# A hybrid decoder layer on one core: norm factors by GpSimd's power in place of a square root and a reciprocal

## The chip, the core and the metric

The kernel runs on one core of a Trainium2 chip. The metric is the device time of one execution in microseconds. Before the change it is 2195.67 us, the median of 3 runs (2195.48 to 2197.35).

## What is computed

One decoder layer over 512 positions of width 2048 in float32. The input is normalised and goes through one projection to four mixers (a gated delta rule with four heads, an RG-LRU, a spatial gating unit and a short convolution). The outputs of the mixers are normalised, joined and projected back, and a gated channel mixer follows. What the change touches are the norms of the mixers' outputs:

```python
def rms_norm(x, w):
    y = xf * lax.rsqrt(jnp.mean(xf * xf, axis=-1, keepdims=True) + EPS)
    return y * w
# gated delta rule, one norm per head of 128 channels
o = o * lax.rsqrt(jnp.mean(o * o, axis=-1, keepdims=True) + EPS) * norm_w * silu(z)
# the other three mixers, one norm each over 512 channels
y_b = rms_norm(rglru_mixer(...), grp_norm_w[l, 0])
y_c = rms_norm(sgu_mixer(...), grp_norm_w[l, 1])
y_d = rms_norm(short_conv_mixer(...), grp_norm_w[l, 2])
y = concatenate([y_a, y_b, y_c, y_d]) @ w_out
```

## The kernel before

In the mixers, channels lie on the 128 partitions and the 512 positions along the columns, so a tile is 128x512. TensorE multiplies float32 as three products of a high and a low half (`mul3`, lines 209 to 211): for every piece of weights ScalarE rounds the high half (line 159) and VectorE subtracts it to get the low half (line 160), each over 128x1024. There are four buffers for the high halves and four for the low ones.

The steps of the mixers are put in an order written out by hand (`MIXERS`): the projections of the heads (`kqv`), the preparation of one head beside the sequential scan of the head before it (`scan_prep`), the gates of the other mixers, the norms, and the gates of the heads (`z_gate`). Within that, a planner of the framework orders each engine's instructions; each engine then runs its own in that fixed order and waits with semaphores. The input projection is done column block by column block (`gemm_T`); the output projection of a block of 512 columns takes its 16 row blocks in four quarters, first the RG-LRU's, then the spatial gate's, the short convolution's and the heads'.

A norm factor is one number per position. Since channels lie on partitions, the squares are summed over partitions by TensorE against a matrix of ones (`ones_sum`, lines 230 and 231), which leaves the sum on all 128 partitions: 128x512 in PSUM, in a bank (`fx`) of which there is one. From it `inv_sqrt` (lines 240 to 243) makes the factor over the whole 128x512: ScalarE's square root with scale and bias (line 241), then VectorE's reciprocal (line 242). VectorE multiplies the mixer's tile by its weight and the factor (line 592 for a head, line 614 for the four tiles of a group). `inv_sqrt` is called seven times: `gdn_norm` for heads 0 to 3 (line 591) and `norm4` for groups 0 to 2 (line 612).

Elsewhere factors of one to four columns are made by `col_rsqrt` (lines 141 to 145) and in `gdn_prep` (line 474), with a multiply-add on VectorE and GpSimd's power to -0.5. GpSimd also adds up squares (lines 590 and 607), multiplies in the convolution (743) and in the gates (755), and zeroes the scan's tile vn (553).

The scan of a head (`gdn_scan`) goes back and forth between the engines: TensorE's `pws` needs VectorE's state `St` (lines 574 and 576), TensorE's `pss` needs VectorE's `vn` (line 564). In the preparation TensorE's `pn` needs `N` (line 490). In the spatial gate TensorE's `pso` writes the bank `fx`, which VectorE empties at line 724.

Of the kernel before, what the change touches and what calls it, by code (L numbers as in the profile page):

```python
# [7 lines left out]
F32 = mybir.dt.float32  # L8
F32R = mybir.dt.float32r
BF16 = mybir.dt.bfloat16  # L10
AF = mybir.ActivationFunctionType
ALU = mybir.AluOpType
# [3 lines left out]
P = 128  # L16
S = 512
# [3 lines left out]
EPS = 1e-6  # L21
# [35 lines left out]
def trunk(ctx: ExitStack, tc: tile.TileContext, x, xT, cols, rows, gdn_row, sgu_row, w_in, w_ba,  # L57
          lru_wa, lru_wx, sgu_ws, w_out, ffn_up, ffn_down, out):
    nc = tc.nc
    v, a, g, pe = nc.vector, nc.scalar, nc.gpsimd, nc.tensor  # L60
# [3 lines left out]
    const = ctx.enter_context(tc.tile_pool(name="const", bufs=1))  # L64
# [13 lines left out]
    def new(tag, name, dt=F32):  # L78
        return tp.tile([P, S], dt, tag=tag, name=name, bufs=NBUF[tag])
# [7 lines left out]
    def G(name):  # L87
        return new("g", name)

    def acc(name):  # L90
        return ps.tile([P, S], F32, tag="acc", name=name, bufs=3)
# [11 lines left out]
    def small(shape, name):  # L103
        return sp.tile(shape, F32, tag=name, name=name)
# [12 lines left out]
    def col(name, i=0):  # L117
        o, _ = _OFF[name]
        return colt[:, o + i:o + i + 1]
# [12 lines left out]
    half = const.tile([P, 16], F32, name="half")  # L132
    g.memset(half, -0.5)

    a.activation(out=small([P, 1], "warm"), in_=half[:, 0:1], func=AF.Square)
    epsc = const.tile([P, 1], F32, name="epsc")
    g.memset(epsc, EPS)
    epsq = const.tile([P, 1], F32, name="epsq")
    g.memset(epsq, EPS * EPS * P)

    def col_rsqrt(dst, src, scale):
        t = small([P, 16], "crs")
# [84 lines left out]
    def ones_sum(hi, lo, bank):  # L227

        p = bank("psum")
        pe.matmul(p, lhsT=onesr, rhs=hi, start=True, stop=False)  # L230
        pe.matmul(p, lhsT=onesr, rhs=lo, start=False, stop=True)
        return p

    def sum_all(src, bank, tag="t"):
        hi, lo = new(tag, "shi", F32R), new(tag, "slo", F32R)
        a.copy(out=hi, in_=src)
        v.tensor_tensor(out=lo, in0=src, in1=hi.bitcast(F32), op=ALU.subtract)
        return ones_sum(hi, lo, bank)

    def inv_sqrt(r, p, scale, bias):  # L240
        a.activation(out=r, in_=p, func=AF.Sqrt, scale=scale, bias=bias)
        v.reciprocal(out=r, in_=r)
        return r

    def to_row(rc, bank, m=None, tag="t", e=v):
# [15 lines left out]
    for c in range(DC):  # L261
# [10 lines left out]
        for j in range(4):  # L272
# [4 lines left out]
                                   op0=ALU.mult, op1=ALU.subtract)  # L277
# [115 lines left out]
    for t in range(NTT):  # L393
# [21 lines left out]
                    in1=gcum.rearrange("p t h -> p (t h)"), op=ALU.subtract)  # L415
# [169 lines left out]
    def gdn_norm(h):  # L585

        o = o_h[h]
        sq = G("osq")
        a.activation(out=sq, in_=o, func=AF.Square)
        g.tensor_tensor(out=sq, in0=sq, in1=sts[h]["q2"], op=ALU.add)  # L590
        r = inv_sqrt(sq, sum_all(sq, fx, "g"), 1.0 / P, epsq)
        v.scalar_tensor_tensor(out=o, in0=o, scalar=col("gdn_norm"), in1=r, op0=ALU.mult, op1=ALU.mult)

    def in_turn(*steps):
# [6 lines left out]
    tot = [None] * 3  # L601
# [7 lines left out]

    def norm4(i, tiles):  # L610

        r = inv_sqrt(tot[i], sum_all(tot[i], fx, "g"), 1.0 / S, epsc)
        for j in range(4):
            v.scalar_tensor_tensor(out=tiles[j], in0=tiles[j], scalar=col("grp", 4 * i + j), in1=r,
                                   op0=ALU.mult, op1=ALU.mult)
            y[4 + 4 * i + j] = tiles[j]
# [156 lines left out]
    def group_norm(i):  # L773
        norm4(i, (yb, yc, yd)[i])
# [4 lines left out]
    for step, i in MIXERS:  # L779
        if step == "scan":  # L780
            in_turn(gdn_scan(i, sts[i]))
        else:
            {"kqv": kqv, "scan_prep": scan_prep, "lru_gate": lru_gate, "sgu_load": sgu_load, "sgu_v": sgu_v,
             "sgu_u": sgu_u, "sconv": sconv, "gdn_norm": gdn_norm, "group_norm": group_norm,
             "z_gate": z_gate}[step](*([] if i is None else [i]))
# [78 lines left out]
    for t in range(NTT):  # L864
        p = acc("pwo")
# [8 lines left out]
        for d in range(DC):  # L874
            v.scalar_tensor_tensor(out=x1[t][d], in0=x1[t][d], scalar=ry[:, t:t + 1], in1=xr[t, d],
                                   op0=ALU.mult, op1=ALU.add)
# [10 lines left out]
        for d in range(DC):  # L887
# [3 lines left out]
            if d % 2 == 0:  # L891
# [4 lines left out]
                            in1=colt[:, o + 4 * d:o + 4 * d + 4].rearrange("p (k o) -> p k o", o=1)  # L896
# [33 lines left out]
    for j in range(2):  # L930
# [4 lines left out]
                               op1=ALU.subtract)  # L935
        v.scalar_tensor_tensor(out=b21, in0=b11, scalar=-1.0, in1=b21, op0=ALU.mult,
                               op1=ALU.subtract)
# [216 lines left out]
```

## Time and profile before

| | |
|---|---|
| median of 3 runs | 2195.67 us |
| the profiled execution | 2186.26 us, span 2184.6 us |
| mean granted TensorE clock | 0.995 |
| TensorE busy | 2155.5 us, 99% |
| VectorE busy | 1396.8 us, 64% |
| ScalarE busy | 897.0 us, 41% |
| GpSimd busy | 133.1 us, 6% |

Engines in the profile: PE is TensorE, PEld its weight loads, DVE is VectorE, ACT is ScalarE, POOL is GpSimd, SP is SyncE. A row of the timeline gives the start and the duration in us, the engine, the line, the operation, output<-inputs, the shape and how many were merged; in brackets the idle time of the engine before it, and what ended it. The matmuls are pipelined, so a row of 0.39 us overlaps the next one. The mixers run until about 626 us, the projections and the channel mixer after that.

### The profile page before, as it was taken

Reading aid. Unit: us, or ns where it says so; the run is one execution under the profiler, and the core shown is the slowest. Engines: PE = TensorE matmul, PEld = TensorE weight load, DVE = VectorE, ACT = ScalarE, POOL = GpSimd, SP = SyncE. Lnnn points to the kernel's source line nnn. Section 1 sums busy time; section 2 is a strip of 40 time slices with the busy share of each in tenths; the row PEclk is TensorE's granted clock in tenths of the full one; section 3 lists DMA queues with packets and bytes.
Section 4 is the critical chain, followed back from the end, with each engine's and each line's share of the span. In section 5 each row is a group of like instructions: output and inputs, shape, how many; then the busy total and the mean of one; then the engine's idle time right before and its main releaser. Section 6 shows DMA issues by size and latency. Waiting matters only on the chain.

```text
span 2184.6 us, 32153 instructions
## 1 busy us (share of the span) xinstructions
PE 2155.5 (99%) x13226; PEld 1932.2 (88%) x13226; DVE 1396.8 (64%) x1853; ACT 897.0 (41%) x1223; POOL 133.1 (6%) x191
## 2 busy tenths in 40 slices
PE   8999999999999989999999999999999999999997
PEld 7788888888888888999999999999999888888885
DVE  6775454944462386989999999999999322423333
ACT  6554242522332464444445444444445312422222
POOL 0001000100100110000000000000002000100002
PEclk9999999999999999999999999999999999999999
DMA  9232132232232343344344434433446422432233
GB/s 300 68 87 78 58 86 70 78 86 78 87 140 101 133 138 114 104 121 122 110 127 122 123 106 125 126 115 114 121 129 199 174 97 97 168 112 96 96 115 146
DMA packets 316690, 254.85 MB, mean 117 GB/s; under 512 B 10496, under 2 KB 265216, under 8 KB 316032
## 3 DMA queue, kind: packets, MB, share of 16 engines
q1 hardware_dynamic: 304768, 219.24, 32.6%
q0 software_dynamic: 8320, 27.27, 3.4%
q10 hardware_dynamic: 3456, 6.29, 0.8%
q8 instruction: 103, 1.69, 0.3%
q14 instruction: 43, 0.35, 0.0%
HBM read 232.85 MB, written 19.92 MB: 116 GB/s over the span
## 4 chain that ended last, share of the span: by engine, by line
PE 84%; issue 11%; DVE 1%; ACT 1%; DMA 1%; POOL 1%; SPq 0%; DVEq 0%; POOLq 0%; ACTq 0%
PE pT L210 14%; PE pT L211 14%; PE pT L209 14%; PE pB L211 5%; PE pB L210 5%; PE pB L209 5%; PE pd L210 4%; PE pd L211 4%; PE pd L209 4%; PE pwo L211 3%; PE pwo L210 3%; PE pwo L209 3%; PE ptt L442 1%; PE plx L209 1%; PE plx L210 1%
## 5 line engine op out<-in xcount | busy, mean ns | idle before, releaser
L160 DVE TENSOR_TENSOR wlo<-raw,whi 128x1024 fp32r<-128x1024 f32 x378 | 461.6, 1221 | 472.4 <-ACT whi L159 464.6
L159 ACT CAST whi<-raw 128x1024 fp32r<-128x1024 f32 x378 | 396.6, 1050 | 808.5 <-PE pd L211 293.4
L210 PE MATMUL pT<-act_lo,whi 128*128 128x512 f32 (+1 forms) x1032 | 365.7, 354 | 2.4 <-DVE act_lo L900 2.4
L211 PE MATMUL pT<-act_hi,wlo 128*128 128x512 f32 (+1 forms) x1032 | 365.1, 354 | 0.0
L209 PE MATMUL pT<-act_hi,whi 128*128 128x512 f32 (+1 forms) x1032 | 365.1, 354 | 0.0
L211 PE MATMUL pB<-act_hi,wlo 128*128 128x256 f32 x984 | 278.5, 283 | 0.0
L210 PE MATMUL pB<-act_lo,whi 128*128 128x256 f32 x984 | 278.4, 283 | 0.0
L209 PE MATMUL pB<-act_hi,whi 128*128 128x256 f32 x984 | 278.2, 283 | 0.0
L209 PE MATMUL pT<-eh,whi 128*128 128x256 f32 x984 | 277.1, 282 | 0.0
L210 PE MATMUL pT<-el,whi 128*128 128x256 f32 x984 | 277.1, 282 | 0.0
L211 PE MATMUL pT<-eh,wlo 128*128 128x256 f32 x984 | 276.8, 281 | 0.0
L210 PEld LDWEIGHTS pT<-act_lo,whi 128*128 128x128 f32 x1032 | 196.6, 190 | 27.1 <-DVE act_lo L900 2.7
L209 PEld LDWEIGHTS pT<-act_hi,whi 128*128 128x128 f32 x1032 | 196.4, 190 | 25.3 <-issue 1.0
L211 PEld LDWEIGHTS pT<-act_hi,wlo 128*128 128x128 f32 x1032 | 196.6, 190 | 24.7 <-issue 1.0
L159 ACT CAST whi<-s 128x1024 fp32r<-128x1024 f32 x123 | 129.0, 1049 | 185.9 <-DVE s L978 114.2
L211 PE MATMUL pd<-whi,act_lo 128*128 128x512 f32 x512 | 199.4, 389 | 0.0
L210 PE MATMUL pd<-wlo,act_hi 128*128 128x512 f32 x512 | 199.3, 389 | 0.0
L209 PE MATMUL pd<-whi,act_hi 128*128 128x512 f32 x512 | 198.4, 389 | 0.0
L209 PEld LDWEIGHTS pB<-act_hi,whi 128*128 128x128 f32 x984 | 188.8, 192 | 0.0
L211 PEld LDWEIGHTS pB<-act_hi,wlo 128*128 128x128 f32 x984 | 188.7, 192 | 0.0
L210 PEld LDWEIGHTS pB<-act_lo,whi 128*128 128x128 f32 x984 | 188.7, 192 | 0.0
L209 PEld LDWEIGHTS pT<-eh,whi 128*128 128x128 f32 x984 | 185.6, 189 | 0.0
(368 smaller groups left out, 3531.2 us busy)
## 6 DMA issues: line engine op xcount, KB each, us to landing
raw<-in_ffn_up_dram SPq DMA_DIRECT2D x176, 512.0 KB, 3.9
raw<-in_ffn_down_dram SPq DMA_DIRECT2D x88, 512.0 KB, 3.4
raw<-in_w_in_dram SPq DMA_DIRECT2D x86, 512.0 KB, 3.7
raw<-in_w_out_dram SPq DMA_DIRECT2D x32, 512.0 KB, 3.8
gd<-fcv POOLq DMA_DIRECT2D x44, 256.0 KB, 3.8
act_lo<-gd POOLq DMA_DIRECT2D x32, 256.0 KB, 3.8
xs<-in_xT_dram SPq DMA_DIRECT2D x16, 256.0 KB, 6.2
xn<-in_x_dram SPq DMA_DIRECT2D x16, 256.0 KB, 6.1
```

The source lines that it names most:

```text
L159: a.copy(out=hi, in_=r)
L160: v.tensor_tensor(out=lo, in0=r, in1=hi.bitcast(F32), op=ALU.subtract)
L209: pe.matmul(p, lhsT=lt[0], rhs=rt[0], start=first, stop=False)
L210: pe.matmul(p, lhsT=lt[0], rhs=rt[1], start=False, stop=False)
L211: pe.matmul(p, lhsT=lt[1], rhs=rt[0], start=False, stop=last)
L442: pe.matmul(p[:, TS[t]], lhsT=lhsT[:, TS[t]], rhs=rhs[:, TS[t]], start=True, stop=True)
```

## The change

The constants for the bias go. `inv_sqrt` becomes a multiply-add on VectorE, which reads the sum from PSUM and writes it to SBUF, and a power on GpSimd, in place, with the exponent -0.5 read from one column of `half` for all 512 columns. The callers pass the bias as a number.

```diff
-    epsc = const.tile([P, 1], F32, name="epsc")
-    g.memset(epsc, EPS)
-    epsq = const.tile([P, 1], F32, name="epsq")
-    g.memset(epsq, EPS * EPS * P)
 ...
     def inv_sqrt(r, p, scale, bias):
-        a.activation(out=r, in_=p, func=AF.Sqrt, scale=scale, bias=bias)
-        v.reciprocal(out=r, in_=r)
+        v.tensor_scalar(out=r, in0=p, scalar1=scale, scalar2=bias, op0=ALU.mult, op1=ALU.add)
+        g.tensor_tensor(out=r, in0=r, in1=half[:, 0:1].broadcast_to([P, S]), op=ALU.pow)
         return r
 ...
-        r = inv_sqrt(sq, sum_all(sq, fx, "g"), 1.0 / P, epsq)
+        r = inv_sqrt(sq, sum_all(sq, fx, "g"), 1.0 / P, EPS * EPS * P)
 ...
-        r = inv_sqrt(tot[i], sum_all(tot[i], fx, "g"), 1.0 / S, epsc)
+        r = inv_sqrt(tot[i], sum_all(tot[i], fx, "g"), 1.0 / S, EPS)
```

## Rows read from the trace of the kernel before

**Rows 1.** The page, busy us of each engine, share of the span, instructions.

```profile
PE 2155.5 (99%) x13226; PEld 1932.2 (88%) x13226; DVE 1396.8 (64%) x1853; ACT 897.0 (41%) x1223; POOL 133.1 (6%) x191
```

**Rows 2.** Busy times by stretch: length, PE, PEld, DVE, ACT, POOL, PEclk, DMA, GB/s.

```profile
370.00:626.00 256.00, 256.00 (x1259) 215.49 (x1259) 153.41 (x192) 96.09 (x138) 30.81 (x22) 1.00 0.28 79
```

**Rows 3.** Lines 241 and 242: count, ns min/median/max, first and last start.

```profile
L241 ACT ACT_TABLE_LOAD  x5: 1283/1283/1283, 375.0 to 609.1; - x5
...
L242 DVE RECIPROCAL osq<-osq x4: 3344/3353/3354, 377.0 to 611.1; 128x512 f32<-128x512 f32 x4
...
L242 DVE RECIPROCAL nsq<-nsq x3: 3347/3352/3354, 410.9 to 615.5; 128x512 f32<-128x512 f32 x3
```

**Rows 4.** GpSimd's powers (lines 145, 474) and a GpSimd addition (607), same columns.

```profile
L145 POOL TENSOR_TENSOR brs<-crs,half x4: 539/548/556, 293.2 to 304.5; 128x1 f32<-128x1 f32 x4
...
L474 POOL TENSOR_TENSOR rk<-rk,half x4: 1020/1264/1931, 103.2 to 423.4; 128x4 f32<-128x4 f32 x4
...
L607 POOL TENSOR_TENSOR nsq<-nsq x9: 1284/1294/1730, 175.0 to 558.6; 128x512 f32<-128x512 f32 x9
```

**Rows 5.** Timeline of VectorE and GpSimd, 395 to 402 us.

```profile
395.67 0.68 DVE L319 SCALAR_TENSOR_TENSOR kT<-th,gconv 128x512 f32<-128x512 f32 x1
...
400.71 1.30 POOL L590 TENSOR_TENSOR osq<-osq,q 128x512 f32<-128x512 f32 x1 [8.81 <-ACT osq L589]
400.83 1.72 DVE L319 SCALAR_TENSOR_TENSOR qT<-th,gconv 128x512 f32<-128x512 f32 x1
```

**Rows 6.** Timeline of VectorE around the seven reciprocals.

```profile
377.00 3.35 DVE L242 RECIPROCAL osq<-osq 128x512 f32<-128x512 f32 x1 [0.78 <-ACT osq L241]
...
382.31 0.75 DVE L724 SCALAR_TENSOR_TENSOR so<-pso,colt,bt 128x512 f32<-128x512 f32 x1
...
410.93 3.35 DVE L242 RECIPROCAL nsq<-nsq 128x512 f32<-128x512 f32 x1 [0.29 <-ACT nsq L241]
...
418.52 0.28 DVE L574 COPY St<-pss 128x128 f32<-128x128 f32 x1
...
424.40 3.35 DVE L242 RECIPROCAL nsq<-nsq 128x512 f32<-128x512 f32 x1
...
428.35 0.29 DVE L564 TENSOR_TENSOR vn<-u,pws 64x128 f32<-64x128 f32 x1
...
435.52 1.12 DVE L490 SCALAR_TENSOR_TENSOR N<-pkk,cb,DN 128x128 f32<-128x128 f32 x4
...
524.28 3.35 DVE L242 RECIPROCAL osq<-osq 128x512 f32<-128x512 f32 x1 [1.31 <-ACT osq L241]
...
531.43 0.35 DVE L576 SCALAR_TENSOR_TENSOR St<-St,gl,pss 128x128 f32<-128x128 f32 x1 [1.54 <-PE pss L571]
...
611.14 3.35 DVE L242 RECIPROCAL osq<-osq 128x512 f32<-128x512 f32 x1 [1.66 <-ACT osq L241]
...
615.54 3.35 DVE L242 RECIPROCAL nsq<-nsq 128x512 f32<-128x512 f32 x1 [0.25 <-ACT nsq L241]
...
623.20 1.21 DVE L160 TENSOR_TENSOR wlo<-raw,whi 128x1024 fp32r<-128x1024 f32 x1
```

**Rows 7.** Timeline of TensorE, instructions that need a VectorE step of rows 6.

```profile
386.23 0.50 PE L722 MATMUL pso<-wsT,vt 128*128 128x128 f32 x3
...
420.61 0.39 PE L563 MATMUL pws<-St,wT 128*128 128x128 f32 x2
...
431.10 0.39 PE L571 MATMUL pss<-vn,kg 128*128 128x128 f32 x2
...
438.33 0.61 PE L448 MATMUL pn<-ident,N 128*128 128x128 f32 x4
...
536.04 0.39 PE L563 MATMUL pws<-St,wT 128*128 128x128 f32 x2
...
626.89 1.07 PE L209 MATMUL pwo<-whi,act_hi 128*128 128x512 f32 x4
```

**Rows 8.** Busy times by stretch, columns as in rows 2.

```profile
799.00:814.00 15.00, 11.33 (x61) 10.19 (x62) 14.90 (x21) 8.78 (x15) 0.46 (x1) 0.66 0.00 0
```

## The prediction

> **What bounds the kernel now.** I read the page's engine shares first: TensorE is busy 99% of the span, VectorE 64%, ScalarE 41%, GpSimd 6% [rows 1]. Then the busy times of the one stretch in which all seven norm factors are made, from 370 to 626 us: TensorE is busy for 256.0 of 256 us at full clock, VectorE for 153.4, ScalarE for 96.1, GpSimd for 30.8 [rows 2]. So TensorE is the bound here. Nothing that ScalarE or VectorE saves can shorten this stretch; only what makes TensorE stop can change the time. The question is therefore what the new GpSimd instruction takes, who waits for it, and how far TensorE can run on without that waiter.
>
> **What is removed.** Seven square roots on ScalarE with five table loads of 1.28 us, and seven reciprocals of 3.35 us on VectorE [rows 3], 23.5 us of VectorE in all. TensorE waits for none of them (it has no gap in the stretch), so the gain is put at nothing. Two small memsets at the start go too, also at nothing.
>
> **What is added on VectorE.** Seven multiply-adds that read the sum from PSUM. The trace of before has none; the nearest row is a VectorE step of the same size that reads PSUM, 0.75 us at 382.31 [rows 6]. It stands where the reciprocal stood and is shorter than it.
>
> **What is added on GpSimd.** Seven powers over 128x512. The trace has powers only of one column, 0.548 us (median), and of four columns, 1.020 us for the undisturbed ones [rows 4]. Three more columns cost 0.472 us, 157 ns each. The lower bound is the nearest row of the full size: a GpSimd addition over 128x512, 1.29 us [rows 4]. The upper bound is the power's own slope: 0.548 + 511 x 0.157 = 80.9 us. The two are a factor of 60 apart. I take 80.9 us, because the rows of the same operation are nearer to it than a row of another operation: if the power went at the rate of the addition, four columns could not cost 0.47 us more than one. What could still bring it down is a loop that handles many columns faster than four; that is a rival below.
>
> The Trainium skill, GPSIMD Engine Reference, section 3.1 (Elementwise), puts a two-input GpSimd operation at about 2.6 cycles of 1.2 GHz per element; for 512 columns that is an estimate of 1.1 us, and by it the change would cost nothing. The addition's row bears that rate out, the power's rows do not.
>
> **Who waits.** The power's result goes to VectorE, which runs its instructions in order: behind the waiting multiplication (line 592 or 614) stand the low halves of the weights (line 160), the copies out of PSUM and the small steps of the delta-rule scan, and TensorE waits for those. Even if the planner puts other VectorE work ahead of that multiplication, the ports get in the way: a VectorE step of 0.68 us with two inputs in SBUF took 1.72 us when it began 0.12 us after a GpSimd addition of 1.30 us, ending 0.54 us after that one ended [rows 5]. So I take VectorE as stopped from the start of a power to its end, but for steps that read PSUM. Behind it on GpSimd's own queue stand the sums of squares (line 607), the convolution's multiplication (743), the zeroing of vn (553) and the four-column powers of the next head (474); their readers are behind the same stop. The weight loads on the sync queue go on until their buffers are full.
>
> **The sum.** For each stop I take the last VectorE step before it, and the first TensorE instruction that needs a VectorE step behind it; TensorE stops there. VectorE's order is that of before.
>
> Gated norm of head 0: multiply-add at 377.00, power from 377.75 to 458.7. Next on VectorE are three steps that end 2.7 us after the reciprocal did (the one at 382.31 ends at 383.06) [rows 6], so 461.4. TensorE reaches the instruction that needs the bank which this step empties at 386.23 [rows 7]. Lost: 75.2.
>
> The next three come close together, and GpSimd does one after the other. Group 0: 410.93, power from 411.7 to 492.6; the state copy that TensorE needs at 420.61 [rows 7] ended 4.5 us after the reciprocal (its row is at 418.52 [rows 6]), so 497.1: 76.5 lost. Head 1: the multiply-add is next, power from 497.9 to 578.8; one split of weights (1.2 us, as at 623.20), then the multiply-add for group 1 at 580.0, whose power ends at 661.6. In between only the multiplication of head 1 and the vn step get through, at 581.6; TensorE, which needs vn at 431.10, is 150.5 behind. N, needed at 438.33, ended 8.0 us after vn [rows 6, 7], so 669.6: 231.3 behind for the three.
>
> Head 2: 524.28, power from 525.0 to 605.9, then the steps up to the state copy. That ended 4.2 us after the reciprocal, of which 1.5 was a wait for TensorE and 0.3 the vn step, which comes through earlier; I take 2.2, so 608.1. TensorE needs it at 536.04 [rows 6, 7]. Lost: 72.1.
>
> Head 3 and group 2: 611.14, power to 692.8, the multiplication, the second multiply-add, power from 694.3 to 775.2. The first weights of the output projection's third quarter were split 5.5 us after the second reciprocal ended (the row at 623.20 [rows 6]), so 780.7. TensorE has work for the first two quarters until 626.89 [rows 7]. Lost: 153.8.
>
> Together 75.2 + 231.3 + 72.1 + 153.8 = 532 us, 76 a power. To this comes the clock. In 15 us near 800 us in which TensorE worked for 11.3 only, the granted clock was 0.66 in the mean [rows 8], that is partly the lower of its two levels (1.2 instead of 2.4 GHz): 0.34 x 15, some 5 us of work. Each of the four stretches that ends a stop pays that once (inside the group of three TensorE would run dry again anyway): 4 x 5 = 20 us. Sum: 552 us.
>
> The profiled execution took 2186.3 us (span 2184.6 and 1.7 around it); the median of the runs is 2195.7. By the profiled one 2738, on the median 2748. I give 2748.
>
> **The rivals.** First, the stop does not hold VectorE: the planner puts the multiplications late, and a power, which computes long between its reads, keeps the ports less than an addition does. Then GpSimd alone sets the end: 377.8 + 7 x 80.9 = 944, and the output projection's third quarter starts near 950 instead of 626.9. That gives +323 and a few us of clock, near 2525. For it: the results of the first powers are needed late. Against it: the short multiplication stands right behind each reciprocal now, and rows 5 show the ports held to the end of an instruction.
>
> The Trainium skill, SBUF — State Buffer, section Who interferes with whom, says the pair of ports shared by VectorE and GpSimd is locked for the whole instruction against a VectorE step with two SBUF inputs. The 1.72 us step agrees for an addition; no row here shows it for a power.
>
> Second, the power is cheaper per column beyond four, at a half or a quarter of the slope: 40.6 or 20.6 us each. The loss per power falls from 76 to 36 or 16, in all +250 or +110, with the clock near 2465 or 2320. For it: no row is wider than four columns. Against it: the two rows already leave a fixed part of 0.39 us aside.
>
> Third, on the other side: the power runs at the addition's rate, 1.3 to 2 us. TensorE's reserve decides: at the tightest place, the group of three, 3 x 80.9 - 231.3 = 11.4 us, 3.8 us a power, so below 7 ns per column nothing is lost. It then would be 2195, no change, since no TensorE gap is there to be won. Against it stand the power's rows.
>
> Fourth, wide powers cost more than the slope: above 2800.
>
> **How the numbers follow.** Forecast 0.68 (own range 2690 to 2800: 4 us more or less per power, the clock between nothing and twice my figure); ports free 0.10; cheaper per column 0.12; addition's rate 0.07; dearer 0.03. The range 2450 to 2800 holds the forecast, the first rival and the half price of the second: 0.8. Measurement can tell 0.2%, some 4 us. Slower by more has 0.93, within it 0.06, faster 0.01.
>
> **What would show it.** Seven GpSimd rows at line 238 of the new kernel of some 81 us each; VectorE idle or stretched under each; TensorE idle in four blocks of about 75, 230 (in three parts), 72 and 154 us between 386 and some 1180 us, with the lower clock behind each; the stretches after it unchanged. A power of another length makes the sum wrong in proportion; VectorE's weight splits at their usual 1.2 us under a running power would make the ports wrong; multiplications far behind their power would make the order wrong.

## The result

The changed kernel takes 2631.37 us (median of 4 runs, 2629.51 to 2636.63) against 2195.57 for the kernel before beside it: 1.198 times as long, 95% interval 1.197 to 1.200, or 436 us more. The forecast was 2748, the range 2450 to 2800.

The page of the changed kernel, engine shares and four rows of the 40 slices (65.7 us each; busy tenths, granted clock in tenths):

```profile
PE 2172.8 (83%) x13226; PEld 1939.9 (74%) x13226; DVE 1380.6 (53%) x1853; ACT 874.0 (33%) x1208; POOL 702.6 (27%) x196
...
PE   9999995304299100899999999999999999999997
...
DVE  5755442101134100337788898899899872242323
...
POOL 0000039999907999102000000000000020010002
PEclk9999998656699555999999999999999999999999
```

TensorE had 99% of the span before [rows 1] and has 83% now; GpSimd went from 133 to 703 us. The hole in TensorE's row lies under the nines in GpSimd's row, between 376 and 1060 us; VectorE is nearly idle there too: only GpSimd is busy, and the others wait. TensorE's own busy time grew by 17.3 us (2155.5 to 2172.8) with the same 13226 instructions; the granted clock fell to 0.5 in the hole, and I put these 17 us down to it.

The new line 238 (count, ns min/median/max, first and last start), which stands where [rows 3] had the reciprocals:

```profile
L238 POOL TENSOR_TENSOR osq<-osq,half x4: 81926/81940/82371, 376.4 to 894.1; 128x512 f32<-128x512 f32 x4
L238 POOL TENSOR_TENSOR nsq<-nsq,half x3: 81910/81915/82380, 462.2 to 976.0; 128x512 f32<-128x512 f32 x3
```

81.9 us each, 574 us for the seven. Who made TensorE wait between 360 and 1100 us (us in all, times, longest):

```profile
PE pwo L205 <- ACT act_hi L787: 156.8, 1, 156.8
PE psum L226 <- ACT shi L232: 128.2, 3, 59.6
PE pT L205 <- DVE scv L740: 80.0, 1, 80.0
PE pT L205 <- DVE rk L471: 49.8, 1, 49.8
```

Together 415 us, and 17 of clock: the 436 us but for a few. (The spans of the two profiled executions differ by 443; the other 11 are short waits.) The view names the last link only. What lies behind it is in GpSimd's timeline:

```profile
376.39 81.94 POOL L238 TENSOR_TENSOR osq<-osq,half 128x512 f32<-128x512 f32 x1 [7.60 <-DVE osq L237]
...
459.52 1.70 POOL L586 TENSOR_TENSOR osq<-osq,q 128x512 f32<-128x512 f32 x1
...
462.19 82.38 POOL L238 TENSOR_TENSOR nsq<-nsq,half 128x512 f32<-128x512 f32 x1
544.55 1.26 POOL L603 TENSOR_TENSOR nsq<-nsq 128x512 f32<-128x512 f32 x1
545.76 82.37 POOL L238 TENSOR_TENSOR osq<-osq,half 128x512 f32<-128x512 f32 x1
628.11 1.26 POOL L739 TENSOR_TENSOR scv<-scv,rb 128x512 f32<-128x512 f32 x1
...
714.90 1.45 POOL L470 TENSOR_TENSOR rk<-rk,half 128x4 f32<-128x4 f32 x1
```

and in TensorE's, at the end of the stops (the bracket is the idle time before the instruction):

```profile
461.93 0.80 PE L226 MATMUL psum<-shi,onesr 128*128 128x512 f32 x1 [31.22 <-ACT shi L232]
...
546.50 0.80 PE L226 MATMUL psum<-shi,onesr 128*128 128x512 f32 x1 [59.63 <-ACT shi L232]
...
630.57 0.80 PE L205 MATMUL pT<-act_hi,whi 128*128 128x512 f32 x1 [80.00 <-DVE scv L740]
...
718.22 0.76 PE L205 MATMUL pT<-act_hi,whi 128*128 128x512 f32 x1 [49.79 <-DVE rk L471]
...
890.61 0.80 PE L226 MATMUL psum<-shi,onesr 128*128 128x512 f32 x1 [37.34 <-ACT shi L232]
```

Each stop ends a few us after a power did. Before each of the first five, GpSimd had a small piece of work to do that it had before the change too: an addition of squares (459.52, 544.55, and one at 888.20), the convolution's product (628.11), the four-column power (714.90). They were queued behind a power of 82 us. Only the last stop, which ends at 1060.44, waits for a power's result itself. VectorE's rows show a second queue behind the powers:

```profile
415.29 1.22 DVE L156 TENSOR_TENSOR wlo<-raw,whi 128x1024 fp32r<-128x1024 f32 x1 [4.21 <-ACT whi L155]
...
628.17 1.75 DVE L588 SCALAR_TENSOR_TENSOR o<-o,colt,osq 128x512 f32<-128x512 f32 x1 [76.87 <-POOL osq L238]
629.84 0.68 DVE L740 TENSOR_TENSOR scv<-pT,scv 128x512 f32<-128x512 f32 x1
...
713.74 3.73 DVE L610 SCALAR_TENSOR_TENSOR so<-so,colt,nsq 128x512 f32<-128x512 f32 x4 [43.20 <-POOL nsq L238]
...
717.99 0.17 DVE L471 RECIPROCAL rk<-rk 128x4 f32<-128x4 f32 x1
```

The splits of weights, with two inputs in SBUF, run at their usual 1.2 us in the middle of a power, so VectorE's ports were not held. But its order did make it stand: at each of the seven powers it came to the multiplication that needs the result (lines 588 and 610) and waited there, for 25.5, 55.6, 76.9, 43.2, 34.5, 68.5 and 80.4 us, 385 in all. It had run on for 56, 27, 6, 39, 47, 13 and 2 us under them. At the first four stops TensorE stood first, by up to 2 us.

So two queues stand behind each power. At the stops at the sums (31.2, 59.6 and 37.3 us) the link goes past VectorE: GpSimd adds, ScalarE rounds, TensorE multiplies. (The low half of the same sum is VectorE's, and the second time it came another 2.5 us later, behind the multiplications.) At the stops of 80.0 and 49.8 us the reader is a VectorE step that stands behind the waiting multiplications; it ran 0.5 and 1.6 us after GpSimd had its piece ready. Which of the two queues sets a stop can't be read from rows that one power's end releases within 5 us.

### The profile page after: what moved, and what is told of

It reads as the page before. It is cut to its first block, busy times and chain, and to the rows that moved or that the text cites. A ratio compares the mean times of both kernels' runs of the same rounds, so it can differ in the third digit from the quotient of the medians.

```text
span 2627.8 us, 32134 instructions
## 1 busy us (share of the span) xinstructions
PE 2172.8 (83%) x13226; PEld 1939.9 (74%) x13226; DVE 1380.6 (53%) x1853; ACT 874.0 (33%) x1208; POOL 702.6 (27%) x196
## 4 chain that ended last, share of the span: by engine, by line
PE 39%; issue 35%; POOL 11%; DVE 6%; DMA 5%; ACT 2%; DVEq 0%; SPq 0%; POOLq 0%; ACTq 0%
POOL nsq L238 6%; PE pT L207 5%; PE pT L206 5%; PE pT L205 5%; DMA raw<-in_ffn_up_dram 5%; POOL osq L238 4%; PE pd L205 3%; PE pd L207 3%; PE pd L206 3%; PE pwo L205 2%; PE pwo L206 2%; PE pwo L207 2%; DVE s L974 1%; DVE wlo L156 1%; PE pB L206 1%
## 5 line engine op out<-in xcount | busy, mean ns | idle before, releaser
L238 POOL TENSOR_TENSOR osq<-osq,half 128x512 f32<-128x512 f32 x4 | 328.2, 82044 | 16.9 <-DVE osq L237 16.9
L916 POOL DMA_DIRECT2D gd<-fcv x44 | 23.8, 541 | 864.0 <-DVE fcv L915 864.0
L238 POOL TENSOR_TENSOR nsq<-nsq,half 128x512 f32<-128x512 f32 x3 | 246.2, 82068 | 0.0
L205 PE MATMUL pwo<-whi,act_hi 128*128 128x512 f32 x224 | 89.2, 399 | 157.5 <-ACT act_hi L787 156.8
```

What stands on the lines that cost most here:

```text
L205: pe.matmul(p, lhsT=lt[0], rhs=rt[0], start=first, stop=False)
L238: g.tensor_tensor(out=r, in0=r, in1=half[:, 0:1].broadcast_to([P, S]), op=ALU.pow)
L916: nc.gpsimd.dma_start(out=gd[f], in_=vt)
```

## The experiments

Two theories were set against each other. The prediction's: VectorE stops for the whole power, by its order and by the ports. The new one: a power holds nothing but GpSimd's own queue, and TensorE stops where its order reaches something queued there behind a power. The runs decide between them on the ports. On the order they don't, for a reason that is told with the multiplications moved. Times of single runs are compared with the kernel before on the same chip, which took between 2192.4 and 2200.1 us.

### No power at all

```diff
-        g.tensor_tensor(out=r, in0=r, in1=half[:, 0:1].broadcast_to([P, S]), op=ALU.pow)
+        a.activation(out=r, in_=r, func=AF.Sqrt)
+        v.reciprocal(out=r, in_=r)
```

> The multiply-add on VectorE stays, and the factor is then made by ScalarE's square root and VectorE's reciprocal in SBUF; there is no power over 512 columns. If the powers are the whole price, as every theory here has it, the time is that of before, 2195 us, within 4 us, and TensorE has no gap between 370 and 626 us. A rival by which the multiply-add itself or the lost bias constants cost something would give a time 5 to 20 us above it.

2188.62 us against 2192.4, ratio 0.9984 (0.9974 to 0.9995): 4 us less, within the 0.2% that can be told from no change. So the whole loss is the powers'. What the few us come from was not looked into. Busy times from 370 to 626 us (columns as in [rows 2]):

```profile
370.00:626.00 256.00, 256.00 (x1260) 215.64 (x1259) 156.58 (x197) 95.96 (x138) 29.90 (x22) 1.00 0.29 80
```

TensorE has no gap, as in [rows 2].

### The price by columns

```diff
+    widths = [8, 16, 32, 64, 128, 256, 512]
 ...
+        n = widths.pop(0)
 ...
-        g.tensor_tensor(out=r, in0=r, in1=half[:, 0:1].broadcast_to([P, S]), op=ALU.pow)
+        if n < S:
+            a.activation(out=r[:, n:], in_=r[:, n:], func=AF.Sqrt)
+            v.reciprocal(out=r[:, n:], in_=r[:, n:])
+        if n:
+            g.tensor_tensor(out=r[:, :n], in0=r[:, :n], in1=half[:, 0:1].broadcast_to([P, n]), op=ALU.pow)
```

> The seven powers are done over the first 8, 16, 32, 64, 128, 256 and 512 columns, in the order head 0, group 0, head 1, group 1, head 2, head 3, group 2; the other columns are made by square root and reciprocal. If the price is linear (0.39 us and 0.157 to 0.16 us per column), the durations are 1.7, 2.9, 5.5, 10.6, 20.9, 41.4 and 82 us. If wide powers went by a faster loop with a step somewhere, the durations would bend; a power of 64 columns in 5 us, say. For the total: only the last two powers lie where TensorE runs dry, 41 and 82 us in a row against 164 with the change, of which 10 us were covered: 157 - 41 = 116 us of gap and some 5 us of clock, near 2317 us (2300 to 2330). If VectorE were held for each power, as the prediction had it, some 10 us more for the 128-column power of head 2, and 10 to 20 for those before it: 2335 to 2350.

GpSimd's timeline, and TensorE's one long wait:

```profile
376.19 1.65 POOL L245 TENSOR_TENSOR osq<-osq,half 128x8 f32<-128x8 f32 x1 [7.60 <-DVE osq L240]
...
426.13 10.52 POOL L245 TENSOR_TENSOR nsq<-nsq,half 128x64 f32<-128x64 f32 x1 [2.35 <-DVE nsq L240]
...
609.38 41.13 POOL L245 TENSOR_TENSOR osq<-osq,half 128x256 f32<-128x256 f32 x1 [6.70 <-DVE osq L240]
650.48 81.92 POOL L245 TENSOR_TENSOR nsq<-nsq,half 128x512 f32<-128x512 f32 x1
```

```profile
PE pwo L205 <- ACT act_hi L794: 108.7, 1, 108.7
```

A straight line: (81.92 - 1.65) / 504 = 0.159 us per column from 8 to 512. The rows of one and four columns before the change [rows 4] already had the slope to 1.5%. The time was 2297.45, 105 more than before beside it, with one gap of 108.7 us in the stretch. That is just below the 2300 to 2330 that was expected for the linear price, and 2335 to 2350 was expected with VectorE held. The power of 128 columns (20.73 us) cost no visible gap.

### One power only

```diff
+    widths = [512, 0, 0, 0, 0, 0, 0]
 ...
```

> Only head 0's factor comes from the power over 512 columns, the other six by square root and reciprocal. Theory of the queues (a power does not hold VectorE's ports; TensorE stops only when its own order reaches a result that stands behind the power on GpSimd's queue, here the sum of squares of head 1, or behind the waiting multiplication on VectorE): a gap of about 31 us as in the changed kernel, and 3 to 5 us of clock, 2225 to 2240 us. Theory of the prediction (VectorE stopped from the start of the power to its end): 75 us and 5 of clock, near 2275.

2237.79 us, 45 more than before. The first wait of TensorE:

```profile
PE psum L226 <- ACT shi L232: 31.2, 1, 31.2
```

The same 31.2 us and the same link as in the changed kernel, and not the prediction's 75. The rest of the 45 is TensorE's busy time, which grew by 10.7 us (2155.5 to 2166.2), and a few small waits. VectorE stands for the same 25.54 us at its multiplication here, so this run does not tell the two queues apart.

### As long, but of multiplications

```diff
-        g.tensor_tensor(out=r, in0=r, in1=half[:, 0:1].broadcast_to([P, S]), op=ALU.pow)
+        a.activation(out=r, in_=r, func=AF.Sqrt)
+        v.reciprocal(out=r, in_=r)
+        for _ in range(63):
+            g.tensor_tensor(out=r, in0=r, in1=ones[:, 0:1].broadcast_to([P, S]), op=ALU.mult)
```

> In place of each power GpSimd multiplies the factor by 1.0, 63 times over 128x512, so that it is as long on GpSimd as a power (63 x 1.25 us, some 79 us and more with disturbances); the factor itself comes from square root and reciprocal. If it is the kind of instruction that decides whether VectorE is held, VectorE's steps with two inputs in SBUF are stretched under the chain (0.68 us to as much as 1.9, 1.22 us to as much as 2.4), as under single additions in the kernel before, while under the power they keep their usual times (1.23 us in the changed kernel). If the length alone decided, both would look alike. The total is no sharp test, since the planner may rate the chain otherwise than the power: 2550 to 2750 us.

VectorE's groups between 377 and 850 us (busy us, mean ns of one), first with the chain, then in the changed kernel:

```profile
L156 DVE TENSOR_TENSOR wlo<-raw,whi 128x1024 fp32r<-128x1024 f32 x40 | 66.7, 1669 | 36.7 <-ACT whi L155 36.2
```

```profile
L156 DVE TENSOR_TENSOR wlo<-raw,whi 128x1024 fp32r<-128x1024 f32 x36 | 44.1, 1225 | 73.5 <-ACT whi L155 73.3
```

With the multiplications a split takes 1669 ns in the mean, with the powers 1225, as with GpSimd idle. So it is the kind of instruction and not its length that slows VectorE, and a power does not, but for its start (last section). The time, 2486.29, was below the 2550 to 2750 expected. GpSimd's timeline shows its other work slipped in between the short instructions, which can't be done with one long one; that this is why the time is lower was not tested.

### The squares added up by VectorE

```diff
-            g.tensor_tensor(out=sq, in0=sq, in1=tot[i], op=ALU.add)
+            v.tensor_tensor(out=sq, in0=sq, in1=tot[i], op=ALU.add)
```

and the same for the squares of a head (the line shown is that of the groups).

> The changed kernel, but the squares of the norms are added up by VectorE and no longer by GpSimd. In the changed kernel three of the six stops of TensorE (31, 62 and 37 us) end with a sum over partitions whose input waits for such an addition, queued behind a power on GpSimd. If GpSimd's queue is what makes these three, they shrink or go and the time falls by 60 to 130 us, to 2500 to 2570. If VectorE's waiting multiplication sets them as well (the next thing to be late), TensorE stops a little later for that and the time stays within 25 us of 2631.

2621.02 us, 429 more than before: the time hardly moved, which speaks against GpSimd's queue. The waits of TensorE leave both open:

```profile
PE pT L205 <- DVE cb L474: 225.0, 1, 225.0
...
PE pT L205 <- DVE scv L740: 38.5, 1, 38.5
PE pss L567 <- DVE vn L564: 29.4, 1, 29.4
```

The stops at the sums are gone, and new ones stand at cb, scv and vn, which need the four-column power, the convolution's product and the zeroing: all still on GpSimd. In its timeline the four-column power comes right behind three powers in a row. But on VectorE four waiting multiplications stand in front of cb as well, and they are done later:

```profile
710.02 1.00 POOL L470 TENSOR_TENSOR rk<-rk,half 128x4 f32<-128x4 f32 x1
```

```profile
710.08 3.74 DVE L610 SCALAR_TENSOR_TENSOR so<-so,colt,nsq 128x512 f32<-128x512 f32 x4 [80.36 <-POOL nsq L238]
...
713.83 0.13 DVE L474 TENSOR_TENSOR cb<-beta,rk 128x4 f32<-128x4 f32 x1
```

Whether VectorE's waiting multiplication sets the stop or GpSimd's queue is left open by this run.

### The multiplications moved, GpSimd's other work moved, and both

In the first kernel the multiplications by the factors go to the end of the mixers in the program, in the second GpSimd's additions, products and zeroings of the mixers go to VectorE (its small powers stay), the third has both edits. Of each edit a part is shown; the groups' multiplications go behind the last gate.

```diff
-        r = inv_sqrt(sq, sum_all(sq, fx, "g"), 1.0 / P, EPS * EPS * P)
-        v.scalar_tensor_tensor(out=o, in0=o, scalar=col("gdn_norm"), in1=r, op0=ALU.mult, op1=ALU.mult)
+        r_h[h] = inv_sqrt(sq, sum_all(sq, fx, "g"), 1.0 / P, EPS * EPS * P)
 ...
+        v.scalar_tensor_tensor(out=o, in0=o, scalar=col("gdn_norm"), in1=r_h[h], op0=ALU.mult, op1=ALU.mult)
         g.tensor_tensor(out=y[h], in0=y[h], in1=z, op=ALU.mult)
```

```diff
-        g.memset(vn, 0.0)
+        v.memset(vn, 0.0)
 ...
-        g.tensor_tensor(out=cv, in0=cv, in1=rb, op=ALU.mult)
+        v.tensor_tensor(out=cv, in0=cv, in1=rb, op=ALU.mult)
 ...
```

> The changed kernel with the multiplications by the factors moved to the end of the mixers, and GpSimd's other work left on GpSimd. With the two kernels that have GpSimd's other work on VectorE it makes four of one kind. If VectorE's wait for the power is all that lengthens the chain of powers, this is as fast as the kernel with both edits, 2520 (2510 to 2540). If TensorE is stopped by GpSimd's queue as well (squares, convolution products and the zeroing of vn behind a power), gaps between the powers remain and the time is 2560 to 2630.

> The changed kernel with GpSimd's additions, products and zeroings of the mixers given to VectorE, and the multiplications where the changed kernel has them. If VectorE's waiting multiplication alone can stop TensorE as long as GpSimd's queue did, the time stays near that of the kernel with only the additions moved, 2590 to 2640. If GpSimd's queue was what mattered, 2520 to 2560.

> The changed kernel, with the multiplications by the factors moved to the end of the mixers (heads with their gates, groups after the last gate) and GpSimd's additions, products and zeroings of the mixers given to VectorE, so that GpSimd has little but the powers. Then nothing waits for a power in mid-course, and the last power's end sets the start of the output projection's third quarter: 376 + 7 x 82 = 950 against 627 before, 6 us from the power to the first product, some 5 us of clock, in all 330: 2515 to 2535. If a power held VectorE's ports, TensorE would stop under each power all the same and the time would stay above 2600.

| | multiplications in place | at the end of the program's mixers |
|---|---|---|
| GpSimd's other work on GpSimd | 2631.37 (+436) | 2634.66 (+435) |
| on VectorE | 2534.12 (+334) | 2519.99 (+328) |

In brackets the difference to the kernel before beside it. The two columns are alike, but that shows nothing of the multiplications: only the program's lines moved. The planner, which orders each engine's instructions, put them back. In the first kernel VectorE's instructions come in the order of the changed kernel all through the powers, and it stands at the same multiplications for the same time:

```profile
627.82 1.75 DVE L755 SCALAR_TENSOR_TENSOR o<-o,colt,osq 128x512 f32<-128x512 f32 x1 [76.87 <-POOL osq L238]
...
713.39 3.73 DVE L614 SCALAR_TENSOR_TENSOR so<-so,colt,nsq 128x512 f32<-128x512 f32 x4 [43.16 <-POOL nsq L238]
```

The third kernel has VectorE's order of the second in the same way. So each row of the table is one order measured twice, and what VectorE's wait costs by itself stays untested.

Clearing GpSimd's queue is worth 102 us. The planner's answer to it is in that figure: the multiplications behind the first and the second power now come 5 and 16 us after these ended, and TensorE runs on without a gap of note to 590 us, under two powers and half of the third. What is left is the serial chain of powers. In the second kernel the first one starts at 383.07 and the last ends at 958.0, 575 us for seven:

```profile
383.07 81.93 POOL L238 TENSOR_TENSOR osq<-osq,half 128x512 f32<-128x512 f32 x1 [76.49 <-DVE osq L237]
...
876.11 81.91 POOL L238 TENSOR_TENSOR nsq<-nsq,half 128x512 f32<-128x512 f32 x1
```

958 against 626.89 for the projection's third quarter before [rows 7] is +331, and +334 was measured. In the changed kernel the same chain takes from 376.39 to 1058, 682 us: while TensorE stands, it does not produce the input of the next power, and GpSimd idles too. Between the fourth and the fifth power, 713.70 to 805.07, it has 13 us of work; in the second kernel they follow each other at once.

### VectorE waiting in place

```diff
+        for m in pins:
+            pinned.enter_context(tc.issue_after(m.ins))
 ...
```

with pins the multiplications of the step before: VectorE issues all that comes later in the program behind them.

> The changed kernel, with every VectorE instruction that the program has later than a factor's multiplication issued behind that multiplication, so that VectorE waits in place, as the prediction assumed. If the order of VectorE's instructions is what made the prediction too high, the loss is what the prediction's sum gives, 552 us: 2720 to 2760. If GpSimd's queue alone makes the stops, the order on VectorE changes little: 2620 to 2660.

2807.30 us, 615 more than before, 88 a power. The waits of TensorE:

```profile
PE psum L227 <- DVE slo L233: 168.6, 4, 85.6
PE pT L207 <- DVE wlo L156: 166.6, 2, 84.7
```

Now TensorE does wait for weight splits (wlo), by a whole power each time. This is the kernel that the prediction computed, and it came out 63 above its 552; that the edit also takes work from TensorE which it could do ahead is a guess, not shown. So the order of VectorE was a real condition of the sum, and in the changed kernel it held only in part: VectorE waited for the powers' results there for 385 us, here for 564.

### One norm started early

```diff
-          ("lru_gate", 3), ("kqv", 2), ("scan_prep", 1), ("sgu_v", None), ("sgu_u", 0), ("sgu_u", 1),
-          ("gdn_norm", 0), ("sgu_u", 2), ("sgu_u", 3), ("kqv", 3), ("group_norm", 0), ("gdn_norm", 1),
+          ("lru_gate", 3), ("group_norm", 0), ("kqv", 2), ("scan_prep", 1), ("sgu_v", None), ("sgu_u", 0), ("sgu_u", 1),
+          ("gdn_norm", 0), ("sgu_u", 2), ("sgu_u", 3), ("kqv", 3), ("gdn_norm", 1),
 ...
```

on top of both edits above.

> As the kernel with the multiplications at the end, and the norm of group 0 (whose squares are summed up by about 204 us) is started right after the RG-LRU's last gate, so that its power runs where GpSimd is idle. If GpSimd's serial chain is the bound, exactly one power leaves it: 82 us less, 2435 to 2455. If something else set the end, the gain would be smaller, or a new stop of TensorE would show up near 267 us, where the preparation of head 2 uses GpSimd: above 2480.

2513.58 us, only 6 less than with both edits alone, where 82 were expected for a chain that is one power shorter. GpSimd's timeline:

```profile
272.21 81.93 POOL L238 TENSOR_TENSOR nsq<-nsq,half 128x512 f32<-128x512 f32 x1 [76.83 <-issue]
354.11 1.01 POOL L470 TENSOR_TENSOR rk<-rk,half 128x4 f32<-128x4 f32 x1
...
411.43 163.84 POOL L238 TENSOR_TENSOR osq<-osq,half 128x512 f32<-128x512 f32 x2 [50.80 <-DVE osq L237]
```

The early power began at 272 and not at 204, the four-column power of head 2 waited behind it until 354 (it stood at 285.92 before), and GpSimd then idled for 51 us, and later for another 41, because the inputs of later powers came late. The expectation missed. That the delayed four-column power is what made the next power late fits these rows and was not tested, nor was why the early power began so late.

### Three powers only

```diff
+    widths = [0, 512, 0, 512, 0, 0, 512]
 ...
```

> Only the three groups take their factors from the power, the heads by square root and reciprocal. If the loss is a fixed sum per power, as the prediction's sum has it (76 each, and two or three times 5 for the clock): 2430 to 2440. If what counts is how far TensorE's order can run on under each (about 30 to 50 of 82 us early in the mixers, little at the end): 40 + 50 + 75 and some 15 of clock, 2340 to 2390.

The groups take the power, the heads the square root and the reciprocal. 2342.45 us, 142 more than before, 47 a power, at the lower end of what was expected if the reach of TensorE's order under each power counts (2340 to 2390), and far from a fixed 76 a power. The third of TensorE's long waits, 38.0 us, is for the last power; the other two:

```profile
PE pT L205 <- DVE scv L747: 56.7, 1, 56.7
PE pn L451 <- DVE N L493: 40.1, 1, 40.1
```

### The factor once per position

```diff
+    def col_factor(src, scale, bias):
 ...
+        for t in range(NTT):
+            pe.matmul(p[:, 4 * t:4 * t + 4], lhsT=hi[:, TS[t]], rhs=onesr[:, 0:4], start=True, stop=False)
+            pe.matmul(p[:, 4 * t:4 * t + 4], lhsT=lo[:, TS[t]], rhs=onesr[:, 0:4], start=False, stop=True)
+        rc, rp = small([P, NTT], "rcf"), small([P, NTT], "rcp")
+        v.tensor_scalar(out=rc, in0=p[:, 0:4 * NTT].rearrange("p (t c) -> p t c", c=4)[:, :, 0], scalar1=scale, scalar2=bias,
+                        op0=ALU.mult, op1=ALU.add)
+        g.tensor_tensor(out=rp, in0=rc, in1=half[:, 0:NTT], op=ALU.pow)
+        return to_row(rp, fx, tag="g")
```

> The factors are made once per position instead of once per position and partition: the sum over channels goes into four columns by eight small matmuls, the power runs over 128x4, and a product with the identity and the ones spreads the factor over the partitions. If the price is GpSimd's per column and not the use of its power as such, the 436 us are gone but for TensorE's added work: 7 x some 1.5 us, 2195 to 2210. If any wait for GpSimd in this place stops TensorE, 2220 or more.

2223.59 us against 2200.06, ratio 1.0101 (1.0082 to 1.0121): 24 us more, outside the expected 2195 to 2210 and where the rival, that any wait for GpSimd stops TensorE, had put it (2220 or more). The powers of four columns, and the engine shares:

```profile
L252 POOL TENSOR_TENSOR rcp<-rcf,half 128x4 f32<-128x4 f32 x7 | 7.4, 1060 | 52.4 <-DVE rcf L250 52.4
```

```profile
PE 2171.3 (98%) x13282; PEld 1944.5 (88%) x13282; DVE 1379.2 (62%) x1881; ACT 874.4 (39%) x1208; POOL 142.1 (6%) x196
```

The seven powers cost 7.4 us instead of 574 and TensorE is back at 98%. TensorE's own work grew by 15.8 us, and its waits for what is made from these powers come to 7.5 us (4.7 for the spread factor, 2.8 for a multiplication by it). So the rival's mechanism gives the smaller part, and the larger is TensorE's: on the engine that is the bound, even the cheap way round is dearer than the square root and the reciprocal, which lay beside it. The expectation had put TensorE's added work too low.

None of these kernels is faster than the kernel before by more than the measurement can tell.

## Why the prediction was right, and 117 us too high

**The bound** was right: TensorE had no gap, so what was removed gave nothing, and the kernel without powers shows it.

**The price of a power** was right: 80.9 us forecast from the rows of one and four columns, 81.9 measured, linear from 8 to 512. The lower bound, the addition's 1.29 us, was 60 times too low; the row of the same operation at another size was the one to trust. The rivals of a cheaper wide power and of the addition's rate fell with it. The figure that the Trainium skill gives in GPSIMD Engine Reference, section 3.1 (Elementwise), some 2.6 cycles per element, was measured for an addition, and these runs show that it is not one for a power: 159 ns a column.

**Who waits** is the step that failed. It said that VectorE stops from the start of a power to its end, by its ports and by its order.

The ports were wrong: splits took 1.23 us under a power, 1.67 under the chain of multiplications. The Trainium skill, SBUF — State Buffer, section Who interferes with whom, has a VectorE step with two SBUF inputs contend with a GpSimd instruction that reads SBUF, and whoever issues first hold the shared pair for the whole instruction. The additions and multiplications here agree, the power does so for its start only (last section), and the measurement decides.

The order was right in part. VectorE did come to a multiplication that waited for the power, every time, but in four of seven cases only after 27 to 56 us of other work. Under the third, the sixth and the seventh power it stood almost from the start, as the sum had it. When it is forced to stand in place at every power, the loss passes the forecast (+615 against 552).

What the prediction put aside is GpSimd's own queue: the readers of what is queued there "are behind the same stop". For the convolution's product and the four-column power that is so. For the sums of squares it is not: ScalarE reads them for the high half, and three stops of TensorE, 128 us, hang on that link. Clearing GpSimd's queue brings +436 down to +334, and the rest is the chain of powers itself. How the 102 us divide between GpSimd's queue and VectorE's order stays open: no kernel here took VectorE's wait away and left GpSimd's queue, and the one that cleared the queue got another order on VectorE with it.

**The sum**, stop by stop, forecast and measured: head 0 75.2 and 31.2; group 0, head 1 and group 1 together 231.3 and 191.9 (59.6 + 2.5 at the sums, 80.0, 49.8); head 2 72.1 and 37.3; head 3 and group 2 153.8 and 156.8. The last is right because there the result of the power is itself what TensorE needs. The three others are too high by 118 in all, since TensorE ran on under a power for longer than VectorE's supposed stop allowed. The clock was put at 20 and took 17. That the total lay inside the range is in part luck: 2450 to 2800 was wide enough for the forecast and for the first rival, which has another mechanism, and the measured 2631 lies about halfway between the two.

**The first rival** was right on the ports and, for four of the seven powers, on the late multiplications, but took GpSimd for empty otherwise; its 2525 is what the kernels with GpSimd's other work moved reach (2534.12 and 2519.99).

## What to carry to other kernels

An operation's price at a new size comes from rows of the same operation at two other sizes, not from another operation at the same size. When an instruction of some 80 us enters an engine that looked idle at 6%, list what else stands in that engine's queue and who reads it, beside the consumer of the new result: here both stood behind each power, and clearing the queue was worth 102 us. A time that does not move after an edit is no proof against its theory before the waits are read; here the stops had only moved on to the next thing behind the powers. And read the engine's order in the trace after an edit that moves lines: here the program changed and VectorE's instructions did not.

## What the runs showed of the hardware

GpSimd's power goes at 159 ns per column over 128 partitions, with about 0.4 us fixed, from 1 to 512 columns. A power leaves VectorE's two-input steps at their usual time (1225 ns in the mean over the 36 splits between 377 and 850 us), while multiplications on GpSimd stretch them to 1669 ns. A step that begins just behind a power's start is the exception. The multiplication of head 3 began 0.06 us after a power (976.04) and took 1.52 us instead of 0.66 to 0.75; in the kernel with three powers a split began 0.44 us after one (412.02) and took 1.68 instead of 1.23:

```profile
976.10 1.52 DVE L588 SCALAR_TENSOR_TENSOR o<-o,colt,osq 128x512 f32<-128x512 f32 x1 [68.54 <-POOL osq L238]
```

```profile
412.46 1.68 DVE L156 TENSOR_TENSOR wlo<-raw,whi 128x1024 fp32r<-128x1024 f32 x1
```

Both come out as an estimate of some 0.9 us from the power's start to where the step goes on (0.06 + 1.52 less 0.66 to 0.75, and 0.44 + 1.68 - 1.23). In the changed kernel all 28 splits that lie more than 2 us inside a power took 1.21 to 1.23 us.

A GpSimd multiplication with a broadcast column took 1.04 us undisturbed over 128x512, the addition of two full tiles 1.29:

```profile
424.25 1.04 POOL L241 TENSOR_TENSOR nsq<-nsq,ones 128x512 f32<-128x512 f32 x1 [1.59 <-DVE nsq L239]
```

Why the power leaves the ports free after its start, when it too reads 512 columns of SBUF, was not tried.
